# A hybrid decoder layer: the scans of stick-breaking attention are divided at pairs of key tiles, done in place and drawn from one queue

## The chip, the core and the metric

One core of one Trainium2 chip runs the whole layer in a single launch. The metric is device time in microseconds (us), the median of the runs shown. Five engines work side by side, each through its own instructions in a fixed order: TensorE (PE, matmuls and transposes), VectorE (DVE), ScalarE (ACT), GpSimd (POOL) and SyncE (SP, which issues the DMAs). An instruction starts when the ones before it on its engine have started and the semaphores it waits for are set.

## The reference, cut to what matters

One decoder layer on 1024 tokens with a width of 1024: a half feed-forward, two attentions side by side (forgetting attention with 8 heads, stick-breaking attention with 8 heads, head width 64), gates, a projection, a second half feed-forward and a gated embedding. The change touches stick-breaking attention alone:

```python
z = jnp.einsum('bqhd,bkhd->bhqk', qi, k).astype(jnp.float32) * scale
mask = kpos[None, :] < pi[:, None]
log_beta = jax.nn.log_sigmoid(z)
log_1m = jnp.where(mask, jax.nn.log_sigmoid(-z), 0.0)
after = lax.cumsum(log_1m, axis=3, reverse=True) - log_1m
a = jnp.where(mask, jnp.exp(log_beta + after), 0.0)
return jnp.einsum('bhqk,bkhd->bqhd', a.astype(v.dtype), v)
```

For a query t and a key s before it the weight is sigmoid(z) times the product, over all keys between s and t, of sigmoid(-z). That product, run from the right end of a row to its left, is what the scans compute.

## The kernel before

All matmuls take float32 data divided in a high and a low part, so that each product is made of several matmuls. A feed-forward, the gates, the attention and the second feed-forward follow each other. The stage that matters here is `attention`, and in it heads h = 8 to 15, the stick-breaking ones.

A head is four **steps**, c = 0 to 3. In a step, `scores` makes two query tiles of 128 rows, the even one i = 2c and the odd one i = 2c + 1, each against its n = 128 (i + 1) keys. PE multiplies queries and keys into PSUM banks "sc" (L1037, L1038), ACT takes two sigmoids of them, G = sigmoid(-z) and T = sigmoid(z) (L1045, L1046), and POOL clears the upper triangle of the diagonal block of T (L1052). Then DVE scans: G is multiplied up from right to left into a second tile R (all scans are issued at L1013), first the diagonal block with a mask, then the rest; and POOL multiplies T by R (L1060, L1064). A tile with i > 2 is divided in two at `cut`, about its middle: the part `right` and the part `left`. The even tile's parts are issued at once. The odd tile's parts are put in the list `later`, and issued in `apply`.

`apply(prev)` follows in the same step and works on the step before it, which may be the last step of the previous head. From the diagonal down it takes pairs of key tiles: PE transposes the weights T of the pair into one of two PSUM banks "pt" (L1089), ACT copies the high half to a tile PT (L1091), and DVE subtracts it from the bank to get the low half (L1092, called the low), which frees the bank. `values` multiplies PT with v on PE (L1111), two pairs behind the transposes; the last two pairs come at the end. The result is added up by ACT and DVE (L1133, L1134). After each pair's transposes one entry of `later` is issued, so that on DVE a scan part of the odd tile stands behind each low; what is left follows before the last values.

Between these, PE gets **fill**: matmuls of other projections (L799, L807, in the last head L1360), listed for each head in `fill`. Each call of `take` in `scores` and `apply` lets the fill go on until its written costs reach a share of the head's total. The shares of the four steps are `share`; a step has 7, 4, 5 and 6 calls. The fill also brings its own work: weights are loaded, the high part is cast by ACT (L129) and the low part is made by POOL in two halves (L139), and the finished columns of the keys are copied by ACT (L881) and subtracted by DVE (L882).

The order of PE, and for these heads that of the scans, lows and casts on DVE and ACT, is the order in which the program text issues them (`order`, `pe`, `scan`). POOL's order and the rest are set by a scheduler when the program is built. Buffers rotate: two each of "GF" (G) and "RN" (R), four of "T", five of "PT". Before, each query tile takes one GF and one RN.

Of the kernel before, what the change touches and what calls it, by code (L numbers as in the profile page):

```python
# [14 lines left out]
ALU = mybir.AluOpType  # L15
# [3 lines left out]
P = 128  # L19
S = 1024  # L20
# [16 lines left out]
def tile_hybrid_decoder_layer(  # L37
# [6 lines left out]
    nc = tc.nc  # L44
# [967 lines left out]
    def scan(*args):  # L1012
        order("dve", nc.vector.tensor_tensor_scan(*args))  # L1013

    def scores(step, fill, later=None):
        step["pr"] = []
        Q, KH, KL = step["st"]["st"]
        fox = step["fox"]
        for i in (2 * step["c"], 2 * step["c"] + 1):
            n = (i + 1) * P  # L1020
            na, w = seg(n)
            d0 = n - P
            T = slot("T", [P, S])
            if fox:
                m = stat([P, 3], "m")
                l = stat([P, 1], "l")
                fb = step["fb"]["t"]
                nc.gpsimd.tensor_add(T[:, d0:n], fb[:, d0:n], mask_fox[:])
                nm_ = 0
            else:  # L1030
                G = slot("GF", [P, S])
                R = slot("RN", [P, S])
            for a in range(na):
                c0, c1 = a * w, (a + 1) * w
                ps = bank("sc")
                q = Q[:, i * P:(i + 1) * P]
                pe(nc.tensor.matmul(ps[:, :w], q, KH[:, c0:c1], start=True, stop=False))  # L1037
                pe(nc.tensor.matmul(ps[:, :w], q, KL[:, c0:c1], start=False, stop=True))  # L1038
                if fox:
                    for x0, x1, add in ((c0, min(c1, d0), fb), (max(c0, d0), c1, T)):  # L1040
                        if x0 < x1:
                            nc.vector.tensor_tensor_reduce(T[:, x0:x1], add[:, x0:x1], ps[:, x0 - c0:x1 - c0], -1.0, m[:, nm_ - 1:nm_] if nm_ else 3e38, ALU.add, ALU.min, m[:, nm_:nm_ + 1])
                            nm_ += 1
                else:
                    nc.scalar.activation(G[:, c0:c1], ps[:, :w], AF.Sigmoid, scale=-(HD ** -0.5))  # L1045
                    nc.scalar.activation(T[:, c0:c1], ps[:, :w], AF.Sigmoid, scale=HD ** -0.5)  # L1046
            if fox:
                nc.scalar.activation(T[:, :n], T[:, :n], AF.Exp, bias=m[:, nm_ - 1:nm_], scale=-1.0, accum_out=l[:])
                nc.vector.reciprocal(l[:], l[:])  # L1049
                nc.gpsimd.tensor_mul(T[:, :n], T[:, :n], l[:].broadcast_to([P, n]))  # L1050
            else:
                nc.gpsimd.affine_select(T[:, d0:n], T[:, d0:n], [[-1, P]], ALU.is_ge, 0.0, base=-1, channel_multiplier=1)  # L1052
                cut = (i + 1) // 2 * P if i > 2 else 0

                def right(T=T, G=G, R=R, n=n, d0=d0, cut=cut):
                    z0 = max(d0, 1)
                    scan(R[:, z0 - 1:n - 1][:, ::-1], G[:, z0:n][:, ::-1], mask_sb[:, z0 - d0:P][:, ::-1], 1.0, ALU.mult, ALU.max)
                    if d0:
                        scan(R[:, cut:d0 - 1][:, ::-1], G[:, cut + 1:d0][:, ::-1], G[:, cut + 1:d0][:, ::-1], R[:, d0 - 1:d0], ALU.mult, ALU.bypass)
                    nc.gpsimd.tensor_mul(T[:, cut:n - 1], T[:, cut:n - 1], R[:, cut:n - 1])  # L1060

                def left(T=T, G=G, R=R, cut=cut):
                    scan(R[:, 0:cut][:, ::-1], G[:, 1:cut + 1][:, ::-1], G[:, 1:cut + 1][:, ::-1], R[:, cut:cut + 1], ALU.mult, ALU.bypass)
                    nc.gpsimd.tensor_mul(T[:, :cut], T[:, :cut], R[:, :cut])  # L1064
                parts = [right, left] if cut else [right]
                if i % 2 and later is not None:
                    later.extend(parts)
                else:
                    for part in parts:
                        part()  # L1070
            step["pr"].append(T)
            fill()

    def apply(step, fill, later=()):
        c = step["c"]
        v2 = step["v"]["v"]
        hd = step["head"] % 4
        av = bank("av")
        pts = {}

        def transposes(kpair):
            width = 512 if kpair < c else 384
            ps = bank("pt")
            for kb in (2 * kpair, 2 * kpair + 1):
                for j in range(2):
                    if kb == 2 * c + 1 and j == 0:
                        continue
                    col = (kb % 2) * 256 + (j * P if kb < 2 * c + 1 else 0)
                    pe(nc.tensor.transpose(ps[:, col:col + P], step["pr"][j][:, kb * P:(kb + 1) * P], identf[:]))  # L1089
            pt = slot("PT", [P, 2, 512], F32R)  # L1090
            high = nc.scalar.copy(pt[:, 0, :width], ps[:, :width])  # L1091
            low = nc.vector.tensor_sub(pt[:, 1, :width], ps[:, :width], f(pt[:, 0, :width]))  # L1092
            if not step["fox"]:
                order("dve", low)
                order("act", high)
            pts[kpair] = pt

        def values(kpair):
            pt = pts[kpair]
            mm = []  # L1100
            for kb in (2 * kpair, 2 * kpair + 1):
                for b in range(2):
                    c0 = (kb % 2) * 256
                    if kb < 2 * c + 1:
                        mm.append((av[:, 0:256], v2[:, kb, hd, :], pt[:, b, c0:c0 + 256]))
                    else:
                        mm.append((av[:, P:256], v2[:, kb, hd, :], pt[:, b, c0:c0 + P]))
            if kpair == c:
                mm = [mm[0], mm[2], mm[3], mm[1]]
            for i, (o, lh, r) in enumerate(mm):  # L1110
                pe(nc.tensor.matmul(o, lh, r, start=(kpair == c and i == 0), stop=(kpair == 0 and i == 3)))  # L1111

        def turn_and_scan(kpair):
            transposes(kpair)
            if later:
                later.pop(0)()
            fill()

        turn_and_scan(c)
        for kpair in range(c - 1, -1, -1):  # L1120
            turn_and_scan(kpair)
            if kpair + 2 <= c:
                values(kpair + 2)
        for part in later:
            part()
        if c:
            values(1)
        fill()
        values(0)
        Y = step["y"]  # L1130
        hh = step["head"] % 2
        ys = Y["t"][hh * HD:(hh + 1) * HD, c * 256:(c + 1) * 256]
        nc.scalar.copy(ys, av[HD:P, :256])  # L1133
        nc.vector.tensor_add(ys, av[0:HD, :256], ys)  # L1134
        if hh == 1 and c == 3 and step["last"] is False:
            nc.sync.dma_start(yd[Y["idx"]], Y["t"][:])
# [82 lines left out]
    def attention():  # L1219
# [73 lines left out]
        for h in range(16):  # L1293
            fox = h < 8
            if h % 2 == 0:
                idx = fox_pairs[h // 2] if fox else 4 + (h - 8) // 2
                ys[h // 2] = {"t": slot("Y", [P, S]), "idx": idx}
            head = ys[h // 2]["idx"] % 4 * 2 + h % 2
            v = (vf1, vf0, vs0, vs1)[h // 4]
            load_fb(h + 1)  # L1300
            total = sum(u[0] for u in fill[h])
            state = [0.0, 0.0, 0]
            share = (7 / 22, 4 / 22, 5 / 22, 6 / 22) if fox else (0.14, 0.19, 0.29, 0.38)
            gens = [u[1] for u in fill[h]]

            def take(last=False):
                state[0] += total * share[state[2]] / (7, 4, 5, 6)[state[2]]
                while gens and (last or state[1] < state[0]):
                    cost = next(gens[0], None)
                    if cost is None:  # L1310
                        gens.pop(0)
                    else:
                        state[1] += cost
            for c in range(4):
                y0, y1 = Y_AT.get((h, c), ((), ()))
                split_y(*y0)
                load_y(*y1)
                step = {"fox": fox, "c": c, "head": head, "st": stacks[h], "v": v, "y": ys[h // 2], "last": h == 15}
                if fox:
                    step["fb"] = fbs[h]  # L1320
                later = []
                state[2] = c
                scores(step, take, later if prev is not None else None)
                if prev is not None:
                    apply(prev, take, later)
                prev = step
            take(True)
        rest = seq(*[g for _, g in fox_branch[7:]])
# [309 lines left out]
```

## Time and profile before

| | before |
|---|---|
| median of 3 runs | 2287.08 us (2287.04 to 2287.11) |
| profiled execution | 2287.47 us |
| its span | 2285.6 us |
| granted TensorE clock | 1.0 |
| PE busy | 2242.3 us, 98% of the span |
| DVE, ACT, POOL busy | 66%, 44%, 35% |
| scans at L1013 | 160, 142.9 us busy (102.6 and 40.3) |
| stick-breaking heads | about 1123.5 to 1406.6 us of the span |

The lists by line give for each group of instructions the engine, what it writes and reads, the count, busy time and the mean of one, then the engine's idle time ahead of them and what ended it. In the answers in order of time, the first two columns are the start and the length in us; the bracket at the end is idle time of the engine ahead of the row, with the instruction that ended it. Instructions of one kind that follow each other are one row with a count. A matmul's row runs to its modelled end, so that rows overlap: what tells PE's pace is the distance of the starts.

### The profile page before, as it was taken

The page shows a single profiled execution, that of the slowest core. Times are in us where ns is not written, and L with a number is a line of the kernel's source. Part 1 is how long each engine was busy: PE and PEld are TensorE (multiplying, and loading weights), DVE is VectorE, ACT ScalarE, POOL GpSimd, SP SyncE. Part 2 cuts the span into 40 slices and gives each one's busy share as a digit, 9 for nine tenths or more (in the row PEclk, how much of TensorE's full clock was granted, in tenths as well). Part 3 has the DMA queues.
Part 4 walks back from the last instruction along what each step waited for, and adds up shares of the span by engine and source line. Part 5 has one row for each costly group of instructions (what it writes and reads, how often), then busy time and mean ns, then how long its engine had stood idle before and what let it go on. Part 6 is the DMA issues. An engine that isn't in the chain of part 4 may idle for free.

```text
span 2285.6 us, 30594 instructions
## 1 busy us (share of the span) xinstructions
PE 2242.3 (98%) x11402; PEld 1900.6 (83%) x11402; DVE 1498.9 (66%) x2264; ACT 999.5 (44%) x1787; POOL 805.7 (35%) x747
## 2 busy tenths in 40 slices
PE   8999999999999999999999989999999999999999
PEld 6888888888888899998788778888888888888887
DVE  8845454688877336566578786888745555778753
ACT  6333333333365445565656663246333333434431
POOL 2444444300011236566457554500535343200121
PEclk9999999999999999999999999999999999999999
DMA  3232323474233342233223346732423232656132
GB/s 139 102 116 93 115 93 115 174 277 170 84 128 130 120 144 72 64 103 88 70 47 83 93 125 203 263 133 74 138 79 129 79 129 79 252 196 220 62 104 83
DMA packets 184902, 283.87 MB, mean 124 GB/s; under 512 B 27945, under 2 KB 104105, under 8 KB 184754
## 3 DMA queue, kind: packets, MB, share of 16 engines
q1 hardware_dynamic: 184752, 281.92, 37.1%
q8 instruction: 90, 1.47, 0.3%
q14 instruction: 58, 0.48, 0.1%
q10 hardware_dynamic: 2, 0.00, 0.0%
HBM read 189.83 MB, written 75.27 MB: 116 GB/s over the span
## 4 chain that ended last, share of the span: by engine, by line
PE 87%; DVE 7%; ACT 3%; issue 1%; POOL 1%; DMA 1%; SPq 0%; DVEq 0%; ACTq 0%; POOLq 0%
PE ps L556 39%; PE ps L454 21%; PE ps L799 7%; PE ps L1555 4%; PE ps L1360 3%; PE ps L807 3%; DVE RN L1013 3%; PE ps L1111 2%; PE ps L506 2%; PE ps L1089 2%; DVE PT L1092 1%; PE ps L1037 1%; PE ps L1038 1%; PE ps L956 1%; PE ps L228 1%
## 5 line engine op out<-in xcount | busy, mean ns | idle before, releaser
L454 PE MATMUL ps<-H,H 128*128 128x512 f32 x2184 | 497.7, 389 | 1.2 <-DVE X L462 1.2
L454 PEld LDWEIGHTS ps<-H,H 128*128 128x128 f32 x2184 | 409.3, 188 | 86.7 <-issue 2.0
L556 PE MATMUL ps<-H,WL 128*128 128x512 f32 x1116 | 265.0, 389 | 0.8 <-ACT WL L105 0.8
L556 PEld LDWEIGHTS ps<-H,WL 128*128 128x128 f32 x1116 | 209.4, 188 | 44.7 <-ACT WL L105 1.2
L556 PE MATMUL ps<-H,Q 128*128 128x512 f32 x612 | 146.0, 389 | 0.0
L462 DVE SCALAR_TENSOR_TENSOR X<-ps,X 128x512 f32<-128x512 f32 x168 | 109.0, 685 | 50.9 <-PE ps L454 50.9
L556 PEld LDWEIGHTS ps<-H,Q 128*128 128x128 f32 x612 | 114.9, 188 | 23.9
L556 PE MATMUL ps<-X,WL 128*128 128x512 f32 x552 | 132.6, 389 | 0.0
L1092 DVE TENSOR_TENSOR PT<-ps,PT 128x512 fp32r<-128x512 f32 (+1 forms) x160 | 99.9, 630 | 49.6 <-ACT PT L1091 48.8
L139 POOL TENSOR_TENSOR WL<-RAW,WH 128x512 fp32r<-128x512 f32 (+1 forms) x84 | 98.1, 1191 | 67.8 <-ACT WH L129 44.5
L556 PEld LDWEIGHTS ps<-X,WL 128*128 128x128 f32 x552 | 103.6, 188 | 21.5
L1111 PE MATMUL ps<-PT,X 128*128 128x256 f32 (+1 forms) x640 | 103.0, 286 | 15.3 <-DVE PT L1092 11.9
L799 PE MATMUL ps<-WH,H 128*128 128x256 f32 x768 | 115.6, 287 | 0.6 <-ACT PT L962 0.3
L807 PE MATMUL ps<-H,WH 128*128 128x512 f32 x384 | 114.9, 408 | 0.0
L1091 ACT CAST PT<-ps 128x512 fp32r<-128x512 f32 (+1 forms) x160 | 87.1, 549 | 61.6 <-PE ps L1089 60.2
L219 POOL TENSOR_SCALAR ss<-ss 128x1 f32<-128x1 f32 x28 | 8.4, 298 | 297.2 <-ACT WL L215 231.9
L1111 PEld LDWEIGHTS ps<-PT,X 128*128 128x128 f32 x640 | 89.8, 190 | 27.6 <-DVE PT L1092 18.2
L556 PE MATMUL ps<-H,PT 128*128 128x512 f32 x456 | 108.8, 389 | 0.0
L1013 DVE TENSOR_TENSOR_SCAN RN<-GF,RN 128x127 f32<-128x127 f32 (+2 forms) x96 | 102.6, 1068 | 2.5
L799 PEld LDWEIGHTS ps<-WH,H 128*128 128x128 f32 x768 | 101.4, 190 | 2.1 <-ACT PT L962 0.5
L1089 PE MATMUL ps<-identf,T 128*128 128x128 f32 x576 | 90.6, 275 | 11.6 <-DVE PT L1092 9.9
L1050 POOL TENSOR_TENSOR T<-T,l 128x128 f32<-128x128 f32 (+3 forms) x64 | 73.1, 1148 | 78.6 <-DVE l L1049 77.2
(434 smaller groups left out, 4825.4 us busy)
## 6 DMA issues: line engine op xcount, KB each, us to landing
hidden<-PT SPq DMA_DIRECT2D x40, 512.0 KB, 3.1
WH<-in_ffn_w_gate_dram SPq DMA_DIRECT2D x38, 512.0 KB, 5.3
Q<-hidden SPq DMA_DIRECT2D x24, 512.0 KB, 7.1
hidden<-RN SPq DMA_DIRECT2D x22, 512.0 KB, 2.6
KH<-in_ffn_w_up_dram SPq DMA_DIRECT2D x20, 512.0 KB, 6.2
KL<-in_ffn_w_up_dram SPq DMA_DIRECT2D x20, 512.0 KB, 6.9
T<-in_ffn_w_down_dram SPq DMA_DIRECT2D x20, 512.0 KB, 4.2
X<-in_x_dram SPq DMA_DIRECT2D x16, 512.0 KB, 9.5
```

The lines of the kernel that those rows point to most:

```text
L139: ins = eng_lo.tensor_sub(lo[part], raw[part], f(hi[part]))
L454: pe(nc.tensor.matmul(groups[g][t][:], act[:, a, k, t * P:(t + 1) * P], wt[:, b, k, :], start=(fresh and n == 0), stop=(i in (6, 1, 4) and ...
L462: nc.vector.scalar_tensor_tensor(xs, groups[g][t][:], scale, xs, ALU.mult, ALU.add)
L556: pe(nc.tensor.matmul(ps[:], hl[:, a, k, :], rhs(m, b, k), start=(first and i == 0), stop=(final and i == 11), skip_group_check=True))
L799: pe(nc.tensor.matmul(ps[:, :n], hT[t // 4](a, k)[:, (t % 4) * P:(t % 4 + 1) * P], w[k // 4][b][:, k % 4, :n], start=(i == 0), stop=(i == ...
L807: pe(nc.tensor.matmul(ps[:], w[a][:, k, :], hT[half](b, k), start=(i == 0), stop=(i == 23)))
L1013: order("dve", nc.vector.tensor_tensor_scan(*args))
L1089: pe(nc.tensor.transpose(ps[:, col:col + P], step["pr"][j][:, kb * P:(kb + 1) * P], identf[:]))
L1091: high = nc.scalar.copy(pt[:, 0, :width], ps[:, :width])
L1092: low = nc.vector.tensor_sub(pt[:, 1, :width], ps[:, :width], f(pt[:, 0, :width]))
L1111: pe(nc.tensor.matmul(o, lh, r, start=(kpair == c and i == 0), stop=(kpair == 0 and i == 3)))
L1555: pe(nc.tensor.matmul(ps, hT[t // 4](a, k)[:, (t % 4) * P:(t % 4 + 1) * P], pl["w"][d, k // 2][b][:, k % 2, cs], start=(i == 0), stop=(i = ...
```

## The change

It has three parts.

1. **In place, one buffer.** A scan writes its result over G instead of into R. A query tile takes one buffer only, GF for the even tile and RN for the odd one. The product that stood at R[s] now stands at G[s + 1], and POOL reads it there.
2. **Divided at pairs of key tiles, in a queue.** Instead of `right` and `left` there is `part(kp)` for each pair kp of key tiles (256 keys), from the diagonal pair c down to 0. The diagonal part of both tiles is issued at once in `scores`. The others go to the list `pend`, which is kept sorted by step and by pair from the right, for both tiles together, and which lives on from step to step. One entry is taken in `scores` after each tile and one in `apply` after each pair's transposes; besides, all that `apply` is about to transpose within the next two pairs is taken first. `later` and its arguments are gone.
3. **Shares.** The fill's shares of the four steps of a stick-breaking head change from 0.14, 0.19, 0.29, 0.38 to 0.22, 0.20, 0.30, 0.28.

```diff
+    def pop(upto=None):
+
+        while pend and (upto is None or pend[0][:2] <= upto):
+            pend.pop(0)[2]()
+            if upto is None:
+                break
+
+    pend = []
...
             else:
-                G = slot("GF", [P, S])
-                R = slot("RN", [P, S])
+                G = slot(("GF", "RN")[i % 2], [P, S])
...
-                cut = (i + 1) // 2 * P if i > 2 else 0
-
-                def right(T=T, G=G, R=R, n=n, d0=d0, cut=cut):
-                    z0 = max(d0, 1)
-                    scan(R[:, z0 - 1:n - 1][:, ::-1], G[:, z0:n][:, ::-1], mask_sb[:, z0 - d0:P][:, ::-1], 1.0, ALU.mult, ALU.max)
-                    if d0:
-                        scan(R[:, cut:d0 - 1][:, ::-1], G[:, cut + 1:d0][:, ::-1], G[:, cut + 1:d0][:, ::-1], R[:, d0 - 1:d0], ALU.mult, ALU.bypass)
-                    nc.gpsimd.tensor_mul(T[:, cut:n - 1], T[:, cut:n - 1], R[:, cut:n - 1])
-
-                def left(T=T, G=G, R=R, cut=cut):
-                    scan(R[:, 0:cut][:, ::-1], G[:, 1:cut + 1][:, ::-1], G[:, 1:cut + 1][:, ::-1], R[:, cut:cut + 1], ALU.mult, ALU.bypass)
-                    nc.gpsimd.tensor_mul(T[:, :cut], T[:, :cut], R[:, :cut])
-                parts = [right, left] if cut else [right]
-                if i % 2 and later is not None:
-                    later.extend(parts)
-                else:
-                    for part in parts:
-                        part()
+
+                def part(kp, T=T, G=G, n=n, d0=d0):
+                    c0 = kp * 256
+                    c1 = min(c0 + 256, n)
+                    z0 = max(c0, 1)
+                    if c1 == n:
+                        z1 = max(d0, 1)
+                        g = G[:, z1:n][:, ::-1]
+                        scan(g, g, mask_sb[:, z1 - d0:P][:, ::-1], 1.0, ALU.mult, ALU.max)
+                        if z0 < d0:
+                            g = G[:, z0:d0][:, ::-1]
+                            scan(g, g, g, G[:, d0:d0 + 1], ALU.mult, ALU.bypass)
+                        c1 = n - 1
+                    else:
+                        g = G[:, z0:c1][:, ::-1]
+                        scan(g, g, g, G[:, c1:c1 + 1], ALU.mult, ALU.bypass)
+                    nc.gpsimd.tensor_mul(T[:, c0:c1], T[:, c0:c1], G[:, c0 + 1:c1 + 1])
+                part(step["c"])
+                pend.extend((step["id"], -kp, lambda kp=kp, part=part: part(kp)) for kp in range(step["c"] - 1, -1, -1))
+                pend.sort(key=lambda e: e[:2])
+                pop()
...
         def turn_and_scan(kpair):
             transposes(kpair)
-            if later:
-                later.pop(0)()
+            pop()
+            pop((step["id"], 2 - kpair))
             fill()
 
+        pop((step["id"], 1 - c))
         turn_and_scan(c)
...
-        for part in later:
-            part()
...
-            share = (7 / 22, 4 / 22, 5 / 22, 6 / 22) if fox else (0.14, 0.19, 0.29, 0.38)
+            share = (7 / 22, 4 / 22, 5 / 22, 6 / 22) if fox else (0.22, 0.2, 0.3, 0.28)
```

More of the change, by code (lines that the diff above doesn't have):

```diff
@@ L1013, in scan, with scores @@
         order("dve", nc.vector.tensor_tensor_scan(*args))
-    def scores(step, fill, later=None):
+    def pop(upto=None):
[4 more added lines that the diff above has]
+    pend = []
+    def scores(step, fill):
         step["pr"] = []
@@ L1071, in scores, with apply @@
+                part(step["c"])
+                pend.extend((step["id"], -kp, lambda kp=kp, part=part: part(kp)) for kp in range(step["c"] - 1, -1, -1))
+                pend.sort(key=lambda e: e[:2])
+                pop()
             step["pr"].append(T)
             fill()
[L1074 removed]
+    def apply(step, fill):
         c = step["c"]
@@ L1317, in attention @@
                 load_y(*y1)
-                step = {"fox": fox, "c": c, "head": head, "st": stacks[h], "v": v, "y": ys[h // 2], "last": h == 15}
+                step = {"fox": fox, "c": c, "head": head, "st": stacks[h], "v": v, "y": ys[h // 2], "last": h == 15, "id": 4 * h + c}
                 if fox:
                     step["fb"] = fbs[h]
-                later = []
                 state[2] = c
-                scores(step, take, later if prev is not None else None)
+                scores(step, take)
                 if prev is not None:
-                    apply(prev, take, later)
+                    apply(prev, take)
                 prev = step
```

## The prediction

> **What bounds the kernel now.** I read the page first (busy shares, the chain that ended last), then the waits and the busy time of the stick-breaking heads, then the instructions of one head in order of time.
>
> ```profile
> span 2285.6 us, 30594 instructions
> PE 2242.3 (98%) x11402; PEld 1900.6 (83%) x11402; DVE 1498.9 (66%) x2264; ACT 999.5 (44%) x1787; POOL 805.7 (35%) x747
> PE 87%; DVE 7%; ACT 3%; issue 1%; POOL 1%; DMA 1%; SPq 0%; DVEq 0%; ACTq 0%; POOLq 0%
> ```
>
> PE sets the time; only where it waits can this change act. The waits from 1125 to 1400 us (total, times, longest), and the busy time of the four steps of head 11 and of all stick-breaking heads:
>
> ```profile
> DVE RN L1013 <- ACT GF L1045: 8.9, 17, 1.2
> PE ps L1111 <- DVE PT L1092: 9.0, 13, 1.0
> PE ps L1089 <- DVE PT L1092: 6.5, 7, 1.8
> ACT GF L1045 <- DVE RN L1013: 1.1, 1, 1.1
> ```
> ```profile
> 1226.64:1233.56 6.92, 6.86 (x49) 5.95 (x47) 4.66 (x9) 3.60 (x9) 4.83 (x7) 1.00 0.58 143
> 1233.56:1238.16 4.60, 4.60 (x26) 3.90 (x25) 2.91 (x6) 2.95 (x7) 1.56 (x3) 1.00 0.07 16
> 1238.16:1246.01 7.85, 7.85 (x46) 6.86 (x46) 7.12 (x12) 5.83 (x13) 5.68 (x7) 1.00 0.29 67
> 1246.01:1259.57 13.56, 11.30 (x60) 9.02 (x59) 11.86 (x12) 6.82 (x14) 9.53 (x9) 1.00 0.35 79
> 1123.50:1406.60 283.10, 265.47 (x1574) 227.53 (x1573) 227.89 (x317) 168.10 (x361) 171.77 (x200) 1.00 0.38 105
> ```
>
> Columns: length, PE, PEld, DVE, ACT, POOL. PE idles 283.10 - 265.47 = 17.6 us here, and 9.0 + 6.5 = 15.5 us of that ends with L1092, the low half of a transposed tile ("the low" below). That is the stake. In head 11 it all lies in step 3 (13.56 - 11.30 = 2.26 us); DVE is busy 11.86 of its 13.56. DVE's order there, and PE's:
>
> ```profile
> 1248.18 1.20 DVE L1013 TENSOR_TENSOR_SCAN RN<-GF,mask_sb 128x128 f32<-128x128 f32 x1 [1.08 <-ACT GF L1045]
> 1249.42 1.86 DVE L1013 TENSOR_TENSOR_SCAN RN<-GF,RN 128x383 f32<-128x383 f32 x1
> 1251.20 0.66 DVE L882 TENSOR_TENSOR KL<-ps,KH 128x512 fp32r<-128x512 f32 x1
> 1251.79 1.77 DVE L1013 TENSOR_TENSOR_SCAN RN<-GF,RN 128x384 f32<-128x384 f32 x1
> 1253.48 0.53 DVE L1092 TENSOR_TENSOR PT<-ps,PT 128x384 fp32r<-128x384 f32 x1
> 1254.95 1.02 DVE L1013 TENSOR_TENSOR_SCAN RN<-GF,RN 128x383 f32<-128x383 f32 x1
> 1255.88 0.67 DVE L1092 TENSOR_TENSOR PT<-ps,PT 128x512 fp32r<-128x512 f32 x1
> 1256.47 2.01 DVE L1013 TENSOR_TENSOR_SCAN RN<-GF,RN 128x512 f32<-128x512 f32 x1
> ```
> ```profile
> 1254.06 0.66 PE L1089 MATMUL ps<-identf,T 128*128 128x128 f32 x4 [1.26 <-DVE PT L1092]
> 1257.07 1.08 PE L807 MATMUL ps<-H,WL 128*128 128x512 f32 x4
> 1259.11 0.62 PE L1111 MATMUL ps<-PT,X 128*128 128x256 f32 x3 [0.85 <-DVE PT L1092]
> ```
>
> The third transposes wait 1.26 us for the first low, which frees their PSUM bank and stands behind three scans; the last values wait 0.85 us for the third low, behind the 512-wide scan. PE's bracket is idle time; each wait also empties its pipeline.
>
> **What a scan costs.** POOL beside it:
>
> ```profile
> 1241.47 1.44 POOL L1060 TENSOR_TENSOR T<-T,RN 128x383 f32<-128x383 f32 x1 [0.77 <-DVE RN L1013]
> 1247.81 2.66 POOL L139 TENSOR_TENSOR WL<-RAW,WH 128x512 fp32r<-128x512 f32 x2
> 1256.12 1.28 POOL L1060 TENSOR_TENSOR T<-T,RN 128x511 f32<-128x511 f32 x1 [1.11 <-DVE RN L1013]
> ```
> ```profile
> 1234.75 0.42 DVE L1013 TENSOR_TENSOR_SCAN RN<-GF,mask_sb 128x128 f32<-128x128 f32 x1 [0.17 <-ACT GF L1045]
> 1235.21 0.75 DVE L1013 TENSOR_TENSOR_SCAN RN<-GF,RN 128x255 f32<-128x255 f32 x1
> 1236.81 0.56 DVE L1092 TENSOR_TENSOR PT<-ps,PT 128x384 fp32r<-128x384 f32 x1 [0.85 <-ACT PT L1091]
> 1237.73 1.27 DVE L1013 TENSOR_TENSOR_SCAN RN<-GF,RN 128x127 f32<-128x127 f32 x2
> 1238.92 0.67 DVE L882 TENSOR_TENSOR KL<-ps,KH 128x512 fp32r<-128x512 f32 x1
> 1240.57 1.53 DVE L1013 TENSOR_TENSOR_SCAN RN<-GF,RN 128x255 f32<-128x255 f32 x2
> ```
>
> Undisturbed: mask 0.42, 127 wide 0.48 (1.27 for the two less 0.75 and the step between), 255 wide 0.75, 383 wide 1.02; so 0.27 per 128 keys and 0.21 per instruction, and 512 wide 1.29. Beside POOL's products the first comer keeps its pace: the 512 scan started at 1256.47 inside the product of 1256.12 to 1257.40, ran 2.01, and lost 0.72 over an overlap of 0.93, that is 0.77 us per us. At 1241.47 the product started inside a running scan: the scans stayed at 1.53 for two, the product grew from 1.02 to 1.44. Lows, which read PSUM, lose nothing (0.67 at 1255.88). The Trainium skill, page "SBUF — State Buffer", section "Who interferes with whom", says a VectorE instruction with two SBUF inputs and a reading GpSimd instruction exclude each other and the first to start wins. The order agrees with these rows, the full blocking does not (0.72 lost of 0.93).
>
> **The change part by part.** Scans go from 160 to 192, products from 104 to 160 (program order). 32 x 0.21 = 6.7 us more DVE; a product costs 0.17 apiece more (two of 256 at 0.72 or so against one of 511 at 1.28, an estimate from the last POOL row), 56 x 0.17 = 9.5 us more POOL. Cover: DVE has 283.1 - 227.9 = 55 us free, POOL 111. In place, one buffer per tile instead of two: ACT waited once, 1.1 us, for a scan to leave such a buffer, beside a PE that had other work, so I cost it at nothing; the bounds are a gain of 1.1 us and none. No DMA is added, no step passes SP's queue. Whether a scan onto its own input is slower no row shows; the same operands move, so 0; at 0.05 us a scan either way, the step between its own rows (1234.75 + 0.42 to 1235.21), each chain below would move by some 0.2 us, which the bounds hold.
>
> What decides is the order on DVE. Before, the odd tile's scans stood behind the first low of apply. After, they stand ahead of it in every step: even mask, a 256 part, odd mask, 128, another 256 part, and only then the first low; after that a low and a part take turns. Walked for head 11, clocks from PE's first scores of the step, 0.23 us a fill matmul (1257.07: 1.08 less one tail of 0.39, by 3). ACT's rows for when the odd tile's sigmoid ends, and step 0:
>
> ```profile
> 1235.32 0.60 ACT L1045 ACTIVATE GF<-ps 128x512 f32<-128x512 f32 x1 [0.29 <-ACT T L1046]
> 1249.81 0.67 ACT L1045 ACTIVATE GF<-ps 128x512 f32<-128x512 f32 x1
> ```
> ```profile
> 1229.49 0.66 PE L1089 MATMUL ps<-identf,T 128*128 128x128 f32 x4
> ...
> 1237.71 0.62 PE L1111 MATMUL ps<-PT,X 128*128 128x256 f32 x4
> ```
> ```profile
> 1226.86 2.66 POOL L139 TENSOR_TENSOR WL<-RAW,WH 128x512 fp32r<-128x512 f32 x2
> 1227.24 0.42 DVE L1134 TENSOR_TENSOR Y<-ps,Y 64x256 f32<-64x256 f32 x1 [0.47 <-ACT Y L1133]
> ```
>
> - Step 3: fill ahead of the third transposes falls from 18 matmuls to 14, so PE wants them at (1254.06 - 1.26 - 1246.01) - 0.92 = 5.9. The sigmoid ends at 1250.48, 4.5, less one matmul 4.2; then 0.42 + 0.48 + 0.75 + 0.56 = 2.2, so 6.4 bare, 7.0 with one overlapped product: idle 0.5 to 1.1, I take 0.9. Two parts and two lows (2.8) later, 9.3 to 9.8, the last low is there about when PE has done 0.45 of transposes, two values and six fill matmuls: no second wait. 2.26 becomes 0.9.
> - Step 1 (no idle now): PE reaches the values at 1237.71, 4.15, plus two more fill matmuls 4.6. The sigmoid ends at 2.4 + 0.23 = 2.6; mask, 128, 255, KL of L882 (0.67, ahead of the low in half of the heads), low: 4.8 without KL, 5.5 with, 0.45 more under a product. A new wait of 0.2 to 1.3, I take 0.7.
> - Step 0: the third transposes now start at 2.85; with four more fill matmuls PE wants them at 3.7. DVE: L1134 ends at 1.0, mask, the last 255 part of the head before, mask, 127, low: 2.6, so 3.65 bare: idle 0 to 0.6, I take 0.3. But the two weight splits of L139 stand there in heads 10, 11 and 13 (before too: 1226.86); they start first and stretch mask and part by 0.77 x 2.66 = 2.0 us: idle 2.0 in three heads. (They stand before head 15 too; its fill waits for the tiles of load_y, so I leave it out.)
> - Step 2: PE idles nothing now (7.85 of 7.85). The first low moves behind the odd scans, but only two banks are needed and nothing waits for one: 0, or the half of one stretched scan, 0.3; I take 0.15.
> - The new shares move 1.6 us of fill from step 3 (0.38 to 0.28), mostly into step 0; as work it costs nothing, as cover it is in the sums above. Heads 9, 10 and 15 have more fill (18.1 to 18.2 us against 15.6 by the costs written in the kernel), so 0.4 less idle in steps 1 and 3.
>
> Sum: step 0 5 x 0.3 + 3 x 2.0 = 7.5; step 1 8 x 0.7 - 1.2 = 4.4; step 2 1.2; step 3 7.2 - 1.2 = 6.0; together 19.1 against 15.5 now: +3.6 us. The profiled execution took 2287.47 us (1.9 beside its span), 0.4 above the median of 2287.08: 2291.1, on the median's scale 2290.7.
>
> **The rivals.**
> - The lows come in time (faster). A part that directly follows another starts before that one's product, and the first comer keeps its pace, as at 1241.47; then the bare chains hold: 8 x (0 + 0.2 + 0 + 0.6) = 6.4 us idle, -9.1: 2278. It decides if the low of step 0 ends by 3.7 and that of step 1 by 4.9. Against it: the splits of L139 start on their own clock.
> - The products and splits get in first everywhere (slower). Step 0 2.0 in four heads and 0.6 in four, step 1 1.3, step 2 0.3, step 3 1.3: 33.6 us, +18: 2305. The skill's page, by full blocking instead of 0.77, would stretch every overlap by a third and lead this way: 0.3 x (3 x 2.0 + 16 x 0.45) = 4 us above my sum, 2295.
> - It does not act: what step 3 gives, steps 0 and 1 take to within the 0.2% (4.6 us) that tells a change of this kernel from none: about 2287. For it: 15.5 and 19.1 are close, and both sums rest on terms of half a us.
>
> **How the numbers follow.** My forecast, waits moved from step 3 to steps 0 and 1 at a small loss (2287 to 2295): 0.45. Lows in time: 0.22. First comers against it: 0.15. No effect: 0.18. Range 2280 to 2300, the forecast's own 2286 to 2296. Faster by over 0.2% (below 2282.5): 0.22; slower (above 2291.7): the second rival and over half of the forecast, since the pipeline that a wait empties is not in the sum, 0.40; within: 0.38.
>
> **What would show it.** Idle before the third transposes of step 3 down from 1.26 to below 1.1, and none before its last values; a new wait of PE's values in step 1 ending with the low; in step 0 the third transposes late in the heads where L139 stands there; lengths of step 3 near 10.3, step 0 near 8 to 10. Wrong if DVE's lows of steps 0 and 1 end before PE wants them, or if a scan in place has another pace than 0.42 and 0.75.

## The result, and the profile after

The changed kernel takes 2292.77 us (median of 16 runs, 2290.28 to 2294.04); the kernel before took 2287.79 us in the same comparison (16 runs, 2286.95 to 2290.21). The ratio is 1.0019, 95% interval 1.0011 to 1.0027: slower, by about what can be told from no change. The fastest runs of the two lie 3.3 us apart. The profiled execution took 2293.81 us, 6.3 more than the profiled one of before; I come to the difference below.

The page of the changed kernel, busy time of the engines and the chain that ended last:

```profile
span 2291.9 us, 30736 instructions
PE 2243.6 (98%) x11402; PEld 1903.2 (83%) x11402; DVE 1493.6 (65%) x2296; ACT 999.1 (44%) x1787; POOL 805.8 (35%) x803
PE 87%; DVE 6%; ACT 4%; issue 2%; POOL 1%; DMA 0%; SPq 0%; ACTq 0%; DVEq 0%; POOLq 0%
```

PE still sets the time. DVE has 32 instructions more and is busy 5 us less; POOL has 56 more in the same time. The names have moved by some lines: the low is L1103 now, the transposes L1100, the values L1122, the products L1077. The waits of the stick-breaking heads (total, times, longest), and the windows of the four steps of head 11, of head 15's steps 0 and 1, and of all eight heads (length, then PE, PEld, DVE, ACT, POOL, granted clock):

```profile
PE ps L1100 <- DVE PT L1103: 14.9, 15, 3.0
DVE GF L1013 <- ACT GF L1053: 13.6, 16, 1.1
DVE RN L1013 <- ACT RN L1053: 10.9, 19, 1.9
PE ps L1122 <- DVE PT L1103: 7.0, 7, 2.1
```
```profile
1226.67:1236.21 9.54, 7.89 (x54) 6.78 (x53) 6.83 (x11) 4.02 (x10) 5.91 (x8) 1.00 0.48 112
1236.21:1242.42 6.21, 5.27 (x28) 4.36 (x27) 4.75 (x8) 3.19 (x7) 3.58 (x6) 1.00 0.09 21
1242.42:1250.41 7.99, 7.99 (x45) 6.82 (x45) 6.01 (x10) 5.92 (x13) 4.54 (x8) 1.00 0.22 51
1250.41:1260.49 10.08, 9.22 (x53) 7.64 (x52) 8.54 (x14) 6.13 (x13) 8.29 (x11) 1.00 0.53 104
1359.29:1372.50 13.21, 10.21 (x56) 8.79 (x55) 10.17 (x15) 5.86 (x13) 7.14 (x8) 0.87 0.56 170
1372.50:1380.64 8.14, 6.00 (x30) 4.99 (x29) 8.02 (x12) 4.15 (x9) 5.47 (x8) 0.96 0.26 75
1124.77:1412.20 287.43, 265.34 (x1570) 229.28 (x1569) 219.80 (x349) 167.76 (x360) 174.13 (x256) 0.99 0.37 103
```

The same two windows of head 15 in the kernel before:

```profile
1357.77:1366.82 9.05, 7.23 (x50) 6.16 (x49) 7.94 (x12) 5.01 (x11) 5.67 (x7) 1.00 0.67 176
1366.82:1372.87 6.05, 5.55 (x30) 4.39 (x29) 6.05 (x10) 4.65 (x9) 2.31 (x4) 1.00 0.65 193
```

PE idles 22.1 us in these heads, 17.6 before; 14.9 + 7.0 of it ends with the low, 15.5 before. Summed over the eight heads by step, from the gaps between PE's matmuls (the predicted row holds waits for lows alone, the others all idle time):

| PE idle, us | step 0 | step 1 | step 2 | step 3 | sum |
|---|---|---|---|---|---|
| before | 4.1 | 0.7 | 1.4 | 11.4 | 17.6 |
| before, heads 8 to 14 | 2.3 | 0.2 | 1.4 | 9.7 | 13.6 |
| predicted (waits for lows) | 7.5 | 4.4 | 1.2 | 6.0 | 19.1 |
| after | 8.9 | 6.9 | 0.4 | 6.0 | 22.1 |
| after, heads 8 to 14 | 5.9 | 4.7 | 0.4 | 4.8 | 15.8 |

By length, heads 8 to 14 together took 234.24 us and take 234.52. Head 15 took 48.15 and takes 52.91; and these heads start 1.2 us later, because of a stretch at half clock ahead of them. That is all of the 6.3 us between the two profiled executions: head 15 and the clock.

The wait of step 0 in head 11, then that of step 3, in order of time in the changed kernel:

```profile
1227.36 2.65 POOL L139 TENSOR_TENSOR WL<-RAW,WH 128x512 fp32r<-128x512 f32 x2
1227.94 0.98 DVE L1013 TENSOR_TENSOR_SCAN GF<-GF,mask_sb 128x127 f32<-128x127 f32 x1
1228.85 1.70 DVE L1013 TENSOR_TENSOR_SCAN RN<-RN 128x255 f32<-128x255 f32 x1
1232.03 0.63 PE L1100 MATMUL ps<-identf,T 128*128 128x128 f32 x4 [1.65 <-DVE PT L1103]
```
```profile
1256.48 0.53 DVE L1103 TENSOR_TENSOR PT<-ps,PT 128x384 fp32r<-128x384 f32 x1
1257.16 0.63 PE L1100 MATMUL ps<-identf,T 128*128 128x128 f32 x4 [0.86 <-DVE PT L1103]
1259.32 0.66 DVE L1103 TENSOR_TENSOR PT<-ps,PT 128x512 fp32r<-128x512 f32 x1
1259.93 0.72 PE L1122 MATMUL ps<-PT,X 128*128 128x256 f32 x4
```

Two scans that take 0.42 and 0.75 by themselves took 0.98 and 1.70 beside the two weight splits, which had started first: 1.51 us lost over an overlap of 2.07. That is 0.73 us per us, but the loss is not a fixed rate, though the prediction has it so. Each scan ends when POOL's instruction has ended and its own columns, at 2.1 ns, have passed: the second split ends at 1230.01, 255 columns take 0.54, and the scan ends at 1230.55. In the prediction's row the product ends at 1257.40, 512 columns take 1.08, and the scan ends at 1258.48. In heads 8 to 15 of the kernel before, 44 scans start at least 0.25 us before the end of a single product or split that was running already; each loses the overlap less 0.19 to 0.21 us, which is the fixed part of a scan. So the second comer is held up fully but for that part, and the prediction read its rows wrongly where it set full blocking aside.

In step 3 the third transposes wait 0.86 and the last values do not wait. Head 15 is another matter; DVE, POOL and PE after, then before:

```profile
1359.38 2.78 DVE L106 TENSOR_TENSOR H<-X,H 128x1024 fp32r<-128x1024 f32 x2
1361.04 2.59 POOL L139 TENSOR_TENSOR WL<-RAW,WH 128x256 fp32r<-128x256 f32 x2
1365.57 1.12 DVE L1103 TENSOR_TENSOR PT<-ps,PT 128x384 fp32r<-128x384 f32 x2
1366.24 0.94 PE L1100 MATMUL ps<-identf,T 128*128 128x128 f32 x4 [3.00 <-DVE PT L1103]
1380.05 0.79 PE L1122 MATMUL ps<-PT,X 128*128 128x128 f32 x2 [2.14 <-DVE PT L1103]
```
```profile
1357.18 3.60 DVE L106 TENSOR_TENSOR H<-X,H 128x1024 fp32r<-128x1024 f32 x2
1362.01 0.52 DVE L1092 TENSOR_TENSOR PT<-ps,PT 128x384 fp32r<-128x384 f32 x1
1362.59 0.66 PE L1089 MATMUL ps<-identf,T 128*128 128x128 f32 x4 [1.80 <-DVE PT L1092]
```

Two low halves of the attention's output (L106, `split_y`) stand on DVE ahead of head 15's step 0. Before, the first low came 1.2 us after them (1362.01); after, four scans come between, and the low starts 3.4 us after them.

The granted clock, two windows of 2 us of the kernel before and the same of the changed one:

```profile
1106.00:1108.00 2.00, 1.85 (x12) 1.63 (x11) 1.09 (x4) 0.37 (x1) 0.63 (x1) 1.00 0.80 192
1108.00:1110.00 2.00, 2.00 (x13) 1.76 (x12) 1.68 (x10) 0.93 (x2) 0.00 (x0) 1.00 0.02 4
```
```profile
1106.00:1108.00 2.00, 2.00 (x9) 1.75 (x10) 1.15 (x4) 0.37 (x1) 0.34 (x1) 0.75 0.66 144
1108.00:1110.00 2.00, 2.00 (x7) 1.85 (x6) 1.10 (x6) 0.92 (x2) 0.00 (x0) 0.50 0.01 4
```

The profiled execution of the changed kernel has three stretches of 3.413 us at half clock (near 1107, 1366 and 1380 us); that of before has none, apart from one at the very end, which both have. The first made its step 1.5 us longer (8.46 against 6.94 us), and of the 4.8 us that head 15 takes longer 2.5 are not idle time and fall to the other two: an estimate of 1.2 to 1.5 us each. The runs of one kernel come in groups some 1.5 us apart. The Trainium skill, page "TensorE: Matmul & The Clock Gate", Part 1, gives a free-running window of 4096 cycles, 3413 ns, and half rate after at least one idle window. The length and the half agree; but PE had idled only 1.5, 3.0 and 2.1 us before these stretches.

### The profile page after: what moved, and what is told of

The parts are those of the page before. It is cut to its first block, busy times and chain, and to the rows that moved or that the text cites. A ratio compares the mean times of both kernels' runs of the same rounds, so it can differ in the third digit from the quotient of the medians.

```text
span 2291.9 us, 30736 instructions
## 1 busy us (share of the span) xinstructions
PE 2243.6 (98%) x11402; PEld 1903.2 (83%) x11402; DVE 1493.6 (65%) x2296; ACT 999.1 (44%) x1787; POOL 805.8 (35%) x803
## 4 chain that ended last, share of the span: by engine, by line
PE 87%; DVE 6%; ACT 4%; issue 2%; POOL 1%; DMA 0%; SPq 0%; ACTq 0%; DVEq 0%; POOLq 0%
PE ps L556 39%; PE ps L454 21%; PE ps L799 7%; PE ps L1564 4%; PE ps L1369 3%; PE ps L807 3%; PE ps L1122 3%; PE ps L506 2%; PE ps L1100 2%; DVE RN L1013 2%; PE ps L1045 1%; PE ps L1046 1%; PE ps L956 1%; DVE PT L1103 1%; PE ps L228 1%
## 5 line engine op out<-in xcount | busy, mean ns | idle before, releaser
L1103 DVE TENSOR_TENSOR PT<-ps,PT 128x512 fp32r<-128x512 f32 (+1 forms) x160 | 99.2, 627 | 41.2 <-ACT PT L1102 40.7
L139 POOL TENSOR_TENSOR WL<-RAW,WH 128x512 fp32r<-128x512 f32 (+1 forms) x84 | 98.2, 1191 | 63.3 <-ACT WH L129 43.9
L1122 PE MATMUL ps<-PT,X 128*128 128x256 f32 (+1 forms) x640 | 102.9, 287 | 13.3 <-DVE PT L1103 9.9
L807 PE MATMUL ps<-H,WH 128*128 128x512 f32 x384 | 113.9, 409 | 0.0
L1122 PEld LDWEIGHTS ps<-PT,X 128*128 128x128 f32 x640 | 90.7, 191 | 24.6 <-DVE PT L1103 14.4
L1100 PE MATMUL ps<-identf,T 128*128 128x128 f32 x576 | 90.5, 275 | 19.6 <-DVE PT L1103 18.3
L556 PEld LDWEIGHTS ps<-H,PT 128*128 128x128 f32 x456 | 85.5, 188 | 17.8
```

Source lines behind the costliest of these rows:

```text
L139: ins = eng_lo.tensor_sub(lo[part], raw[part], f(hi[part]))
L556: pe(nc.tensor.matmul(ps[:], hl[:, a, k, :], rhs(m, b, k), start=(first and i == 0), stop=(final and i == 11), skip_group_check=True))
L807: pe(nc.tensor.matmul(ps[:], w[a][:, k, :], hT[half](b, k), start=(i == 0), stop=(i == 23)))
```

## The experiments

My theory: the lows set PE's waits, and a low waits for what the program order puts before it on DVE, stretched where POOL is first. The rivals: it is the shares that matter; the scans in place have a price or a gain of their own; and, once head 15 was seen, that its waits come from its fill.

**The order without the new shares.** The changed kernel with the shares of before:

```diff
-share = ... (0.22, 0.2, 0.3, 0.28)
+share = ... (0.14, 0.19, 0.29, 0.38)
```

> The changed kernel with the old shares of fill (0.14, 0.19, 0.29, 0.38). If the order of scans and lows on VectorE makes the loss: steps 0 and 1 have less cover for the late lows, some 0.9 us a head more idle in step 0 and 0.4 in step 1, and step 3 loses its wait (0.7 a head less): 2292 to 2299 us, no better than the changed kernel. If the new shares make the loss: back to 2287 to 2288.

2298.45 us (ratio to before 1.0049, 1.0037 to 1.0062). The share theory falls: the order is the loss, and the new shares win back 5.7 us of it. Part of that is the clock: this run's profile has five stretches at half clock, and PE's idle time is 23.6 us, only 1.5 above the changed kernel's. Two details of mine were wrong. Step 1 idles less here (4.5 us), not more; and step 3 still idles 6.0 us, of which 1.85 are head 15's first scores waiting for the DMA of their keys.

**The new shares without the order.** The kernel before with the shares of the change:

> The kernel before with the new shares alone. If the order on VectorE makes the loss: the lows of steps 0 and 1 stay in time (idle there no more than before, 4.8 us over the eight heads), but step 3, bound by VectorE, loses up to 1.6 us of cover a head: 2292 to 2300 us by another place than the changed kernel, idle in step 3 from 11.4 to 18 or more. If the shares make the loss of the changed kernel: 2291 to 2293, with the idle time in steps 0 and 1.

2295.17 us (1.0029, 1.0018 to 1.0040). Idle in step 3 rises from 11.4 to 18.7 us; steps 0 and 1 fall to 1.4 and 0. All idle time together rises by 3.3 us, to 21.0. The profiled execution took only 2288.96 us, at a granted clock of 1.000; the other six took 2293.6 to 2295.4 at 0.996 or 0.997. So of the 7.9 us some 6 come with the clock. Neither half of the change is good alone. In the queue the new shares repair step 0 and not step 1: with the old shares heads 8 to 14 idle 11.2 us in step 0 and 1.8 in step 1, with the new ones 5.9 and 4.7.

**In place alone.** The two parts, the order and the shares of before; the scan works on G itself, and the product reads G:

```diff
-scan(R[:, z0 - 1:n - 1][:, ::-1], G[:, z0:n][:, ::-1], mask..., 1.0, ...)
+g = G[:, z0:n][:, ::-1]
+scan(g, g, mask..., 1.0, ...)
...
-nc.gpsimd.tensor_mul(T[:, cut:n - 1], T[:, cut:n - 1], R[:, cut:n - 1])
+nc.gpsimd.tensor_mul(T[:, cut:n - 1], T[:, cut:n - 1], G[:, cut + 1:n])
```

> The kernel before, with its two parts, its order and its shares, but the scans in place in one buffer a tile. If a scan in place has the pace of one into another tile: 2287 to 2288.5 us, scans at 0.42 (mask) and 1.02 (383 or 384 wide) as before. If it is slower in place, or the one buffer makes ScalarE wait: 2289 to 2293.

2281.98 us (0.9977, 0.9968 to 0.9986): 5.3 us faster than before, against all that I expected. Scans by themselves keep their pace, but POOL's products are shorter. PE's idle time falls by about the same, from 17.6 to 12.7. So in the old order this part of the change is a gain of 5 us that I had put at nothing, and the queue with its shares costs 10 to 11 us on top of it.

**Why the products are shorter.** The kernel before, with both its buffers; only, the scan's result is written at the keys' own places and not one lower, so that the product reads R one element further on than T:

```diff
-scan(R[:, z0 - 1:n - 1][:, ::-1], G[:, z0:n][:, ::-1], ...)
+scan(R[:, z0:n][:, ::-1], G[:, z0:n][:, ::-1], ...)
...
-nc.gpsimd.tensor_mul(T[:, cut:n - 1], T[:, cut:n - 1], R[:, cut:n - 1])
+nc.gpsimd.tensor_mul(T[:, cut:n - 1], T[:, cut:n - 1], R[:, cut + 1:n])
```

> Before's kernel, two buffers per tile kept; only the scan's result is written at the keys' own places in R (R[1:n]) and not one place lower, so that the product reads R one element further on than T, as the in-place kernels do. Place theory (the product is faster because its two operands start one element apart): the 512-wide products fall from 1.28 to about 1.09 us and the 383-wide undisturbed ones from 1.00 to 0.86, and the time is that of the scans in place, 2281.5 to 2284. Buffer theory (it is the one buffer per tile, or the scan onto its own input): products stay at 1.28, time 2286.5 to 2288.5.

2281.62 us (0.9972, 0.9963 to 0.9982). Groups of the 512-wide product and scan (count | busy, mean ns | idle before), of before and of this run:

```profile
L1064 POOL TENSOR_TENSOR T<-T,RN 128x512 f32<-128x512 f32 x8 | 10.2, 1279 | 8.1 <-DVE RN L1013 8.1
L1013 DVE TENSOR_TENSOR_SCAN RN<-GF,RN 128x512 f32<-128x512 f32 x8 | 16.1, 2016 | 0.0
```
```profile
L1064 POOL TENSOR_TENSOR T<-T,RN 128x512 f32<-128x512 f32 x8 | 8.7, 1092 | 8.1 <-DVE RN L1013 7.0 <-PE ps L799 1.2
L1013 DVE TENSOR_TENSOR_SCAN RN<-GF,RN 128x512 f32<-128x512 f32 x8 | 14.6, 1820 | 0.0
```

This settles it: it is the place at which the product reads its second operand, one element further on than the first, and neither the single buffer nor the scan onto its own input. The product falls from 1279 to 1092 ns, and the scan that runs beside it loses 0.2 us less.

**The same the other way round.** The changed kernel with the sigmoid written one place lower; the scans follow, and the product again reads equal places (only the sigmoid's lines are shown):

```diff
-nc.scalar.activation(G[:, c0:c1], ps[:, :w], AF.Sigmoid, ...)
+g0 = max(c0, 1)
+nc.scalar.activation(G[:, g0 - 1:c1 - 1], ps[:, g0 - c0:w], AF.Sigmoid, ...)
```

> The changed kernel, in place, in its queue and with its shares; only the sigmoid is written one place lower (key x at x - 1), so that the product reads G and T at equal places, as before's kernel did. Place theory: 255- and 256-wide products go back to 0.73 from 0.64 us undisturbed, the parts are more stretched, and the time rises from 2292.8 to between 2295 and 2300 (the 5.3 us that scans in place gave the kernel before, over a similar number of overlaps). Buffer theory: products stay at 0.64, time 2291 to 2294.

2294.09 us (1.0032, 1.0022 to 1.0042). The mechanism holds, its size does not: the shortest 255- and 256-wide products go from 630 to 720 ns,

```profile
L1077 POOL TENSOR_TENSOR T<-T,RN x78: 630/640/1538, 1128.7 to 1399.4; 128x256 f32<-128x256 f32 x46, 128x255 f32<-128x255 f32 x32
```
```profile
L1078 POOL TENSOR_TENSOR T<-T,RN x78: 720/835/1635, 1127.1 to 1399.6; 128x256 f32<-128x256 f32 x46, 128x255 f32<-128x255 f32 x32
```

(shortest, median and longest ns, of the changed kernel and of this run), but the time rises by 1.3 us between the medians (3.0 by the two ratios to before) and not by 5. By the time alone the buffer theory would fit better; the products decide. DVE's busy time grows by 4.7 us (219.8 to 224.5), against 9.4 between before and the scans in place (227.9 to 218.5). One thing fits: by the rows' start and end times, the scan had started first in 41 of the 73 us in which a product and a scan overlap in this run, and in 18 of 50 us in the kernel before, so more of the price falls on POOL (174.1 to 194.7 us), which has time to spare. That this is the cause is not shown.

**The lows first.** The changed kernel; in steps 0 and 1 the queue is not drawn on in `scores`, and the odd tile's first part waits in it until the first low has been issued:

```diff
+wait = step["c"] < 2 and step["id"] > 32
+if not (wait and i % 2):
     part(top)
+    top -= 1
...
-pop()
+if not wait:
+    pop()
```

> The changed kernel, but in steps 0 and 1 of a head the scores take no part from the queue and the odd tile's diagonal part goes to the queue too, so that it stands behind the first low. If the late lows make the loss: PE's idle time in step 1 falls from 6.9 to under 2 us over the eight heads and in step 0 from 8.9 to 3 to 6, steps 2 and 3 stay near 6.4: 2281 to 2287 us, below the changed kernel and perhaps below the one before. If the shares, the number of scans or the scans in place make it: 2291 to 2293, unchanged.

2314.67 us (1.0122, 1.0107 to 1.0138). Step 1's wait went to 0, as expected, and my total missed by 30 us: parts taken late are parts that the next step's transposes wait for. The transposes' group in this run:

```profile
L1105 PE MATMUL ps<-identf,T 128*128 128x128 f32 x267 | 48.1, 282 | 34.3 <-POOL T L1077 29.6 <-DVE PT L1108 4.0
```

29.6 us now end with POOL's products, where nearly all of the waits ended with a low. Step 2 idles 17.1 us (0.4 in the changed kernel), and step 0, which was to fall, 10.7 (8.9).

**The splits of L139.** The changed kernel; POOL writes zeros where it made the low halves:

```diff
-ins = eng_lo.tensor_sub(lo[part], raw[part], f(hi[part]))
+ins = nc.gpsimd.memset(f(lo[part]), 0.0) if stick and ... else eng_lo.tensor_sub(...)
```

> The changed kernel; in heads 8 to 15 GpSimd writes zeros where it made the low halves of the weights (L139), so it reads no SBUF there (the low halves are left out of what the products of these weights compute). If the splits stretch the scans of step 0 as I reckoned (2.0 us in each of heads 10, 11 and 13; 1.37, 1.65 and 1.81 measured), step 0 idles 0.2 to 0.5 there, and head 15's steps 0 and 1 (3.00 and 2.14) fall below 2.0 and 1.0; PE's idle falls from 22.1 to between 14 and 17 and the time to 2284 to 2288. If the wait of step 0 is only the new order of the scans, its idle stays above 1.2 in these three heads and the time at 2291 to 2294.

2283.21 us (0.9980, 0.9971 to 0.9989), a little below what I had expected. Step 0 of heads 10, 11 and 13 idles 0.38, 0.04 and 0.00 us, where it idled 1.37, 1.65 and 1.81; PE's idle over the eight heads is 15.0. Head 11's step 0 in this run, and a scan beside a memset:

```profile
1223.41:1231.33 7.92, 7.88 (x54) 6.77 (x52) 5.32 (x11) 4.03 (x10) 4.67 (x8) 1.00 0.35 85
```
```profile
1224.09 0.98 POOL L141 MEMSET WL<- 128x512 f32 x2
1224.69 0.40 DVE L1015 TENSOR_TENSOR_SCAN GF<-GF,mask_sb 128x127 f32<-128x127 f32 x1
1225.02 0.71 DVE L1015 TENSOR_TENSOR_SCAN RN<-RN 128x255 f32<-128x255 f32 x1
```

The scan inside the memset loses nothing. The Trainium skill, page "SBUF — State Buffer", section "Who interferes with whom", says that two SBUF inputs of VectorE contend with a GpSimd instruction that reads SBUF, not with one that only writes; these rows agree. The first comer's price is shown. In head 15 only a part of it: 2.61 and 1.63 us of 3.00 and 2.14 remain, above the 2.0 and 1.0 that I had expected.

**Head 15.** The changed kernel, with two of the entries for `split_y` (and the `load_y` beside them) one step earlier: what stood ahead of head 15's step 0 now stands ahead of head 14's step 3, and what stood there ahead of step 2:

```diff
-(14, 3): ((0, 1), (4, 5)), (15, 0): ((2, 3), (6,)), ...
+(14, 2): ((0, 1), (4, 5)), (14, 3): ((2, 3), (6,)), ...
```

> The changed kernel; only the splits of Y (L106) that stood ahead of head 15's step 0 stand ahead of head 14's step 3, and those of that step ahead of step 2. Split theory (head 15's step 0 idles 3.00 us because two low halves of Y, 2.8 us, stand on DVE ahead of all its scans): this idle falls below 1.5, head 15's step 1 does not grow, head 14's steps 2 and 3 take 0 to 1.5 more, and the time falls by 1 to 3 us to 2289.5 to 2292. Share theory (it waits because the new shares put more fill, and so more work of DVE behind the fill, into this step): the idle stays above 2.5 and the time at 2292 to 2294.

2296.02 us (1.0034, 1.0021 to 1.0046). Head 15's step 0 idles 0.46 us where it idled 3.00: the split theory holds for its place. The total missed, by a new wait in head 14's step 2:

```profile
L106 DVE TENSOR_TENSOR H<-X,H 128x1024 fp32r<-128x1024 f32 x3 | 3.6, 1212 | 5.2 <-PE ps L807 5.2
```
```profile
1339.55:1355.20 15.65, 9.75 (x45) 8.03 (x45) 9.75 (x14) 8.66 (x16) 5.84 (x10) 0.77 0.47 151
1366.53:1375.59 9.06, 8.60 (x56) 7.36 (x55) 7.53 (x13) 5.76 (x13) 4.79 (x8) 1.00 0.31 88
```

(DVE's group in that step, then the windows of head 14's step 2 and head 15's step 0.) The split needs a buffer H that fill matmuls of L807 still read. DVE stood 5.2 us behind it, PE idled 5.9, and the clock was halved for 10.24 us from 1348 on. I had costed the move by DVE's time alone and had not asked when its buffer comes free.

**Better than both.** Scans in place in the order of before; besides, in step 3 the even tile's second part goes into the queue, so that the first low stands behind one scan less:

```diff
 if i % 2 and later is not None:
     later.extend(parts)
+elif later is not None and step["c"] == 3:
+    parts[0]()
+    later.extend(parts[1:])
```

> The kernel before with scans in place; besides, in step 3 alone the even tile's second part is queued with the odd tile's parts, so that DVE's first low stands behind a mask scan and one 383-wide scan and not behind one more of 383, and the last part of the odd tile comes behind the last low. Order theory (what a low stands behind sets the wait): idle of step 3 falls from 7.83 to between 1 and 4 us over the eight heads, nothing new in step 0 above 1 us, time 2276 to 2279.5. Rival (the waits only move to the next step, whose transposes want the part that is now last): step 0's idle rises by as much, time 2281 to 2284.

2277.06 us (0.9954, 0.9941 to 0.9966). Step 3 idles 1.95 us where it idled 7.83; step 0 takes back 2.0 (3.5 to 5.5), twice what I had allowed. The 1.95 us all lie in head 14, and hardly any of it is a wait for a low: head 15's first scores wait for the DMAs of their keys:

```profile
1350.54 0.30 PE L1036 MATMUL ps<-KH,Q 128*128 128x128 f32 x1 [1.56 <-DMA KH<-KH]
1351.11 0.33 PE L1037 MATMUL ps<-KL,Q 128*128 128x128 f32 x1 [0.27 <-DMA KL<-KL]
```

Head 11's step 3 has no idle time left:

```profile
1244.20:1254.94 10.74, 10.74 (x60) 9.04 (x59) 9.13 (x12) 6.68 (x14) 8.24 (x8) 1.00 0.43 93
```

On top of it, shares of 0.17, 0.19, 0.29, 0.35 and of 0.20, 0.19, 0.29, 0.32, and the latter with head 15 left at 0.14, 0.19, 0.29, 0.38:

> The fastest kernel so far (scans in place, in step 3 the even tile's second part late; 2277.1) with shares of 0.17, 0.19, 0.29 and 0.35 for the stick-breaking heads in place of 0.14, 0.19, 0.29 and 0.38. If fill in step 0 covers what idles there (5.48 us over eight heads) and step 3, which idles in head 14 alone, has cover to spare: step 0 falls to 3 to 4.5, step 3 stays below 3, time 2275 to 2276.8. If step 0's waits are set by the splits of L139 and move with them: no change, 2276.5 to 2278.

> As the run before, with shares of 0.20, 0.19, 0.29 and 0.32. If cover is what counts: step 0 idles 2 to 4 us, step 3 begins to idle again (2 to 5), time 2275 to 2278; if not, step 3 idles over 4 and the time is above 2278.

> As the run before (scans in place, in step 3 the even tile's second part late, shares 0.20, 0.19, 0.29, 0.32; 2276.0), but head 15 keeps 0.14, 0.19, 0.29, 0.38. With 0.20 its step 0 idled 2.88 us and the head took 48.5 us, with 0.14 it idled 0.33 and took 45.7. If the fill of step 0 there brings the wait: head 15 at 45.5 to 46.5 us, the time 2273 to 2275. If not (the half-clock stretch near 1365 us sets it): 2275.5 to 2276.5.

2276.71, 2276.03 and 2276.12 us. Their runs overlap with each other and with 2277.06, so I can't rank them. Step 0 kept 5.0 and 6.6 us of idle time in the first two, above what I expected; in the second 2.9 of it is head 15. The last run was to show that head 15's fill brings that wait, and missed: its step 0 still idles 3.6 us with the old shares. The traces show another link. Where head 15's first scores wait 1.8 to 2.0 us for the DMAs of their keys (the kernel of 2277.06, that of 2276.71, and the queue with the old shares), its step 0 idles only 0.2 to 0.3 us; in the last two kernels they don't wait for the keys, and step 0 idles 2.9 and 3.6, behind L106 again (3.22 us on DVE in the last). The fastest median, 2276.03, is 0.9947 of before (0.9934 to 0.9961), some 12 us.

## Why the prediction was right or wrong

The number was 2290.7; the runs gave 2290.3 to 2294.0, median 2292.8. It lies within the range and in the forecast's own, on the side that I gave: a loss of 3.6 us forecast, 5.0 between the medians. The mechanism is the one I gave, waits for lows that move from step 3 to steps 0 and 1. That the size came so near is luck, by misses of opposite sign. Waits for lows were to go from 15.5 to 19.1 us and went to 21.9. In heads 8 to 14 they went from 12.7 to 15.6, where my terms give 17.85; in head 15 from 2.8 to 6.3, where they give 1.25. Beside these stand a gain in POOL's products that I had put at nothing, and a loss by the clock that was not in the sum.

- **The stake and the bound: right.** PE's idle time is the waits for the low, 15.5 of 17.6 us before and 21.9 of 22.1 after.
- **The walk through DVE's order: right.** Head 11: step 3 0.9 predicted and 0.86 measured, with no second wait; step 1 0.7 and 0.94; step 2 0.15 and 0. Step 0 in heads 10, 11 and 13: 2.0 predicted, 1.37, 1.65 and 1.81 measured; without the splits next to nothing. The 2.0 was high because the scans came 0.6 us into the splits and not at their start (1227.94 and 1227.36 in head 11).
- **"The full blocking does not", and 0.77 us per us: a wrong reading that did little harm.** 0.72 of 0.93 is the overlap less the fixed 0.2 us of a scan. At this overlap both give the same, and at the 2.07 us of head 11 the rate came out at 0.73. But the price that the second rival takes from full blocking, a third more on every overlap, does not follow: full blocking is what the rows already hold.
- **"In place ... I cost it at nothing", with a gain of 1.1 at most: wrong, the largest miss.** In the order of before it is worth 5.3 to 5.9 us, not through buffers but through the product's operands: the product reads G one place further on than T. I had read the diff's `G[:, c0 + 1:c1 + 1]` as a matter of indices.
- **More busy time, DVE +6.7 and POOL +9.5: wrong.** DVE fell by 8.1 us in these heads (227.89 to 219.80) and POOL rose by 2.4 (171.77 to 174.13): products of 256 take 0.64 and not 0.72 us, and the scans are stretched less. It was covered anyway. That shorter products are part of why heads 8 to 14 waited less than my terms give would fit: with products at equal places again these heads idled 17.7 us, and not 15.8.
- **"They stand before head 15 too; its fill waits for the tiles of load_y, so I leave it out": wrong.** I had 1.25 us of waits for head 15 and it has 6.3. What stands there is L106 on DVE, 2.8 us. Moving it took the 3.00 us of step 0 to 0.46.
- **The clock: not in the sum.** Three stretches at half clock cost about 4 us of the profiled execution; 2293.81 less 4 is near the fastest runs. In the other kernels' profiles, two with PE idle below 16 us (scans in place; no splits) have none, and those above 22 have two to five. But the new shares in the old order idled 21 us in a profile without one, while its other executions were granted 0.996 or 0.997; and kernels with 9 to 12 us have one or two. So idle time alone does not set them; what does, stays open.
- **The rivals.** That the lows come in time fell: steps 0 and 1 wait. That products and splits get in first everywhere fell too: outside the three heads and head 15, step 0 idles 0 to 0.5. That it does not act is near in the total and wrong in the parts: the queue with the scans in place and the old shares costs 11 us, and the shares alone 8, some 6 of these with the clock.

## What to carry to other kernels

When an edit moves an operand by one element, cost the instructions that read it anew, on every engine: here an index was worth as much as the best new order (5.3 and 4.9 us). Before a step is moved earlier on an engine, ask when its output buffer comes free, and who will want what it pushes back; the deferred parts and the earlier splits each cost more than the wait that they took away. And walk the odd one out, the last head with its own work on DVE, with the same care as the typical one, since seven equal heads came out 2.3 us better than forecast and the eighth 5.1 us worse.

## What the hardware showed that I had not expected

- POOL's float32 product of two tiles takes 1279 ns for 512 columns when both are read at the same place, and 1092 when the second starts one element later: 2.1 and 1.8 ns a column, from the 256- and 512-wide ones (739 and 1278, 638 and 1091 ns at the median). Whether it is the difference of the places or the odd place itself was not tried.
- A scan that starts inside a running product or split loses the whole overlap but for its fixed 0.2 us (0.72 of 0.93 us, 0.95 of 1.16), so a short overlap costs it almost nothing and a long one nearly all.
- TensorE's clock was granted at half for stretches of 3.413 us, or two or three such in a row, in some executions and not in others; in the changed kernel after stalls of 1.5 to 3.0 us, and near 1107 us behind a stall of 1.54 us that stands in the kernel before without it.
